# A transformer layer on one core: first gate weights in small tiles, stores ahead of loads at the hand-over, a quarter of x kept as fp32 in memory

## The chip, the cores and the metric

The kernel runs on one core of a Trainium2 chip. The metric is the device time of one execution in microseconds (us). The engines are TensorE (PE in the profile, its weight loads PEld), VectorE (DVE), ScalarE (ACT), GpSimd (POOL) and SyncE (SP), which only issues transfers. Each engine has its own instruction queue, worked off in the order of the program; the engines wait for one another by semaphores.

## The reference, cut to what matters

One encoder layer over 1024 tokens of width 1024, all in fp32:

```python
xn = rms_norm(x, norm_g)
qa, ka, va, za, qb, kb, vb, zb = split(xn @ w_in, 8 groups of 512 columns)
ya = subln(diff_attention(qknorm(qa), qknorm(ka), va)) * silu(za)     # 4 heads, dense, T5 bias
yb = neighbourhood_attention(qknorm(qb), qknorm(kb), vb) * silu(zb)   # 8 heads, 2-D window, learned bias
x  = x + concat(ya, yb) @ w_out
x  = x + sigmoid(x @ w_ple_gate) * (p @ w_ple_proj)
```

## The kernel before

**Precision.** Every large product is made of three TensorE passes in fp32r. A helper splits each operand into a high part (an ACT copy to fp32r) and a low part (a DVE subtraction of the high part from the operand) and multiplies high by high, high by low and low by high. So each tile that TensorE reads costs one ACT and one DVE instruction first.

**Stage 1, projections (0 to 307 us).** The six groups qa, ka, va, qb, kb, vb go as three pairs through a Strassen-like scheme: seven products of half-size blocks for each pair, on blocks and sums of x (A11, A12, A22, S1 to S4) and blocks and sums of w_in. `steps` lists 42 half-products, and the loop at the end of the function body makes one in each iteration `i` (`step_mm`, 24 matmuls, lines L232 to L234), evacuates the one before (`step_evac`), loads weight chunks eight ahead (`w_load`), splits two chunks (`w_split`: ACT L215, DVE L216; chunks `4+2i` and `5+2i`), and runs what `hooks[i]` holds. Hooks 0 to 10 are the work on x: norm, transposes on TensorE (`x_trans`, L368), the block sums and their splits (L357, L358, and on POOL L397), and the small product p @ w_ple_proj (`ple_mm`; its halves are evacuated with a factor 0.5, half 0 on ACT L314, half 1 on DVE L316). Block A21 of x isn't used by the scheme. It is only needed by the gate products later, so `x_trans` splits it for tokens 512 to 1023 (ACT L378, DVE L382; DVE writes a difference into the fp32 copy's own tile), stores both parts to memory, and `x_reload` brings them back, high part in iteration 37, low part in iteration 40.

**The order of transfers.** Nearly all transfers are issued by SP, in the order of the program; one that waits holds up all behind it. Stores are collected in `pst` and issued by `ple_st()`: before the hooks up to iteration 39, after them from iteration 40 on.

**The hand-over (iterations 37 to 43, around 270 to 335 us).** The hooks 35 to 41 load what the neighbourhood attention needs: K, the bias R, Q for the first unit (`load_q`, three transfers), V (`load_v`, three transfers a unit, of 48 or 64 KB each), and the weights of the gates. Gate columns come in eight groups of 128 (`zseq`): `z_load` loads a group's weights into `zraw`, `z_split` makes the high part on ACT (L542) and puts the low part (DVE L545) into the list `zl`, which `z_low()` works off; `z_mm` makes the products (L567 to L569) for tokens 0 to 511 and then 512 to 1023, the second half with A21. The first group's `zraw` lies in the pool of six 4 KB tiles (`TA`) that also holds the projections' results on their way to memory (`C`, `vah`, `sth`, `stl`); its low part is made in iteration 42, when `fill(24)` first calls `z_low()`.

**Stage 2 (307 to 500 us)** interleaves 32 units of neighbourhood attention (scores `na_s` L632, softmax `na_e`, transposes `na_t` L670, values `na_pv`) with the gate products, by the generator `z_stream` and `fill(n)`: 24 matmuls first, then the first unit's scores, six matmuls, the second unit's scores, six matmuls, then the first unit's transposes. Once 24 matmuls of a group are through, `z_stream` puts the next group's high split into ACT's queue. Gate results for the dense attention are stored to `uad`. **Stage 3** is the dense attention, **stage 4** the output projection and the last gate.

Of the kernel before, what the change touches and what calls it, by code (L numbers as in the profile page):

```python
# [7 lines left out]
F32 = mybir.dt.float32  # L8
F32R = mybir.dt.float32r
I32 = mybir.dt.int32  # L10
AF = mybir.ActivationFunctionType
OP = mybir.AluOpType
# [3 lines left out]
P = 128  # L16
# [8 lines left out]
COL = dict(qa=0, ka=512, va=1024, za=1536, qb=2048, kb=2560, vb=3072, zb=3584)  # L25
# [6 lines left out]
def ap_of(t, off, dims):  # L32
    return bass.AP(tensor=t.tensor, offset=t.offset + off, ap=[list(d) for d in dims])
# [7 lines left out]
def layer_kernel(ctx, tc, x, p, ngr, w_in, w_out, gains, lamv, t5p, rpbp, w_gate, w_ple,  # L41
# [9 lines left out]
    def nm(s):  # L51
        cnt[0] += 1
        return f"{s}_{cnt[0]}"

    def T8(shape, dt=F32, n="t8"):
        return sb.tile(shape, dt, name=nm(n), tag="b8", bufs=16)

    def T4(shape, dt=F32, n="t4"):
        return sb.tile(shape, dt, name=nm(n), tag="b4", bufs=8)

    def TA(shape, dt=F32, n="ta"):
        return sb.tile(shape, dt, name=nm(n), tag="a4", bufs=6)

    def T2(shape, dt=F32, n="t2"):
        return sb.tile(shape, dt, name=nm(n), tag="b2", bufs=NB2)
# [17 lines left out]
    def PS(shape, n="ps"):  # L83
        return psp.tile(shape, F32, name=nm(n), tag="ps", bufs=4)
# [4 lines left out]
    def DT(shape, dt=F32, n="d"):  # L89
        n = nm(n)  # L90
        return dr.tile(shape, dt, name=n, tag=n, bufs=1)

    def raw(a):
        return a.bitcast(F32) if a.dtype == F32R else a

    def ld(o, i):
        return nc.sync.dma_start(raw(o), raw(i))  # L97

    def st(o, i):
        return nc.sync.dma_start(raw(o), raw(i))  # L100
# [6 lines left out]
    act = nc.scalar.activation  # L107
    V = nc.vector
# [97 lines left out]
    def w_split(j):  # L206
        if j >= len(chunks):
            return
        pi, n, k = chunks[j]
        r = raws.pop(j)  # L210
        if n == "P1":
            tk["b11", k] = r
        w = T4([P, 2, 512], F32R, n="w")
        wts[chunks[j]] = w
        act(w[:, 0], r, AF.Copy)  # L215
        V.tensor_tensor(w[:, 1], r, w.bitcast(F32)[:, 0], op=OP.subtract)  # L216
# [73 lines left out]
    pst = []  # L290
# [11 lines left out]
    def ple_mm(t, c0=0, c1=2):  # L302
        h, l = phl[t]
        if c0 == 0:
            po[t] = TA([P, D], n="pp")
        o = po[t]
        for c in range(c0, c1):
            cs = slice(c * 512, c * 512 + 512)
            ps = PS([P, 512], "pps")
            for i, (a, w) in enumerate(((h, wph), (l, wph), (h, wpl))):  # L310
                for k in range(2):
                    mm(ps, a[:, k], w[:, k, cs], start=(i + k == 0), stop=(i + k == 3))
            if c == 0:
                act(o[:, cs], ps, AF.Copy, scale=0.5)  # L314
            else:
                V.tensor_scalar(o[:, cs], ps, 0.5, None, op0=OP.mult)  # L316
        if c1 == 2:
            pst.append(lambda: st(ppd[t], o))

    def ple_st():  # L320
        while pst:
            pst.pop(0)()


    XA = {}
    a21d = DT([P, 2, 4, 512], F32R, n="a21")

    def x_tiles(*names):
        for n in names:
# [25 lines left out]
    def split(n, ts, src, low):  # L355
        h, l = XA[n]
        act(h[:, :, ts], src, AF.Copy)  # L357
        low.tensor_tensor(l[:, :, ts], src, h.bitcast(F32)[:, :, ts], op=OP.subtract)  # L358

    def x_trans(t):  # L360
        hat = xhats.pop(t)
        u = t % 4
        ts = slice(u * P, u * P + P)
        pt = [PS([P, 4, P], "xtp") for _ in range(2)]
        for b in range(2):
            for k in range(4):
                kc = 4 * b + k
                nc.tensor.transpose(pt[b][:, k], hat[:, kc * P:(kc + 1) * P], idn)  # L368
        if t < 4:
            split("A11", ts, pt[0], V)  # L370
            split("A12", ts, pt[1], V)
            for b in range(2):
                act(xf[b][:, u], pt[b], AF.Copy)
            return
        s, a21 = xsum[0][:, u], xsum[1][:, u]
        act(a21, pt[0], AF.Copy)
        sp = TA([P, 2, 4, P], F32R, n="a21s")
        act(sp[:, 0], pt[0], AF.Copy)  # L378
        V.tensor_tensor(s, pt[1], a21, op=OP.add)
        split("A22", ts, pt[1], V)  # L380
        V.tensor_tensor(a21, xf[0][:, u], pt[0], op=OP.subtract)
        V.tensor_tensor(sp[:, 1], pt[0], sp.bitcast(F32)[:, 0], op=OP.subtract)  # L382
        split("S1", ts, s, V)
        V.tensor_tensor(s, s, xf[0][:, u], op=OP.subtract)
        pst.append(lambda: st(a21d[:, :, :, ts], sp))

    xsum = []
    xf = []
# [11 lines left out]
        ts, s = xv(t)  # L400
        split("S4", ts, s, V)

    XA["A21"] = []

    def x_reload(i):
        XA["A21"].append(T8([P, 4, 512], F32R, n="xr"))
        ld(XA["A21"][i], a21d[:, i])

    qkd = {n: (DT([4, P, S], F32R, n=n + "h"), DT([4, P, S], F32R, n=n + "l")) for n in ("qa", "ka", "qb", "kb")}
    vad = (DT([S, 512], F32R, n="vah"), DT([S, 512], F32R, n="val"))  # L410
# [118 lines left out]
    zraw = {}  # L529
    zw = {}  # L530

    def z_load(col, T=None):
        r = (T or T4)([P, 8, P], n="zraw")
        ld(r, w_in[:, col:col + P].rearrange("(k q) d -> q k d", q=P))
        zraw[col] = r

    def z_split(col, k0=0, k1=8):
        r = zraw[col]
        if k0 == 0:
            zw[col] = T8([P, 2, 8, P], F32R, n="zw")  # L540
        w = zw[col]
        act(w[:, 0, k0:k1], r[:, k0:k1], AF.Copy)  # L542

        def low():
            V.tensor_tensor(w[:, 1, k0:k1], r[:, k0:k1], w.bitcast(F32)[:, 0, k0:k1], op=OP.subtract)  # L545

        zl.append(low)

    zl = []
    zp = []  # L550

    def z_low():
        while zl:
            zl.pop(0)()
# [44 lines left out]
    def load_q(pr, R):  # L599
        q1 = T4([P, 2, 512], F32R, n="Q1")  # L600
        h, l = qkd["qb"]
        for (dst, s) in ((q1[0:64], h), (q1[64:128], h), (Q2[R][0:64], l)):
            ld(dst, s[pr, :, R * 512:(R + 1) * 512].rearrange("(h d) s -> d h s", h=2))
        qb[pr, R] = q1
# [104 lines left out]
    def na_consts_k():  # L709
        k = T8([P, 2, S], F32R, n="K2")  # L710
        for h in range(2):
            cast(k[64:128, h], pen)
        K2.append(k)
# [8 lines left out]
    def load_r0():  # L722
        t = T8([P, 2, 752], n="R0")
        Rt[0] = [t[:, h] for h in range(2)]
        for h in range(2):
            ld(t[:, h], ap_of(rpbp, h * 23 * 48 + 1, [[48, 8], [1, 16], [1, 752]]))
# [90 lines left out]
    def pre(i):  # L817
        if i >= len(units):
            return
        pr, R, j = units[i]  # L820
        if j == 0:
            if R == 0:
                load_q(pr, 1)
            elif pr + 1 < 4:
                load_q(pr + 1, 0)
        if (R, j) == (0, 2) and pr + 1 < 4:
            load_k(pr + 1)
        if (R, j) == (1, 2) and pr + 1 < 4:
            load_r(pr + 1)
        if i + 2 < len(units):  # L830
            load_v(*units[i + 2])
# [89 lines left out]
    def s7():  # L921
# [3 lines left out]
    NS = len(steps)  # L925
# [7 lines left out]
        30: lambda: u_load(30),  # L933
        31: lambda: u_load(31),
        NS - 7: lambda: (na_consts_k(), load_k(0)),
        NS - 5: lambda: (load_r0(), x_reload(0)),
        NS - 4: lambda: z_load(COL["zb"], TA),
        NS - 2: lambda: (na_consts_q(), load_q(0, 0), load_v(0, 0, 0), load_v(0, 0, 1), z_split(COL["zb"], 0, 4),
                         z_split(COL["zb"], 4, 8), x_reload(1)),
        NS - 1: lambda: (pre(0), z_load(COL["zb"] + P), na_consts_k()),  # L940
    }
    lam_in = []
    normed = []
    for i in range(len(steps) + 2):
        w_sum1(LA - 2 + 2 * i)
        w_sum1(LA - 1 + 2 * i)
        if i < len(steps):
            step_mm(i, 0, 2)
        ready, normed = normed, []
        got = step_evac(i - 1) if 0 < i <= len(steps) else None  # L950
        for n, t0, c, rs in ready:
            qk_norm2(c, rs)
        if got:
            n, t0, c = got
            if n[0] == "v":
                v_evac(n, t0, c)
            else:
                normed.append((n, t0, c, qk_norm1(c)[1]))
        w_sum2(LA - 2 + 2 * i)
        w_sum2(LA - 1 + 2 * i)  # L960
        w_load(LA + 2 * i)
        w_split(4 + 2 * i)
        w_load(LA + 1 + 2 * i)
        if i < NS - 2:
            ple_st()
        if i in hooks:
            hooks[i]()
        if i >= NS - 2:
            ple_st()
        if i < len(steps):  # L970
            step_mm(i, 2, 3)
        if i == len(steps):
            fill(24)
            na_s(*units[0])
            na_e(*units[0])
            na_n(*units[0])
        w_split(5 + 2 * i)
        if i < len(steps):
            step_mm(i, 3, 4)
        for n, t0, c, rs in ready:  # L980
            qk_trans(n, t0, c)
# [464 lines left out]
```

## Time and profile before

| what | value |
|---|---|
| median of 3 runs (lowest to highest) | 844.71 us (844.12 to 845.74) |
| the profiled execution's own time, and its span | 844.99 us, 843.2 us |
| PE busy | 785.1 us, 93% of the span |
| PEld, DVE, ACT, POOL busy | 649.3, 517.9, 435.4, 266.8 us |
| granted clock of TensorE, mean | 0.976 of full speed |
| chain that ended last | PE 65%, DMA 10%, DVE 9%, ACT 5%, issue 5%, POOL 4% |

TensorE is busy for most of the span; the span is its work, plus the times in which it waits, plus what it loses when its clock is at the lower level. Which wait is worth looking for is read from the views of its waits and of short stretches, further down.

### The profile page before, as it was taken

To read this page: it belongs to the slowest core of one execution; us is meant where nothing else is said; L and a number is where in the kernel's file an instruction comes from. 1 tells how busy PE (TensorE), PEld (TensorE's weight loads), DVE (VectorE), ACT (ScalarE), POOL (GpSimd) and SP (SyncE) were. 2 spreads that over 40 slices of the span, in tenths; PEclk is the share of its full clock that TensorE was granted. 3 is DMA by queue.
4 is the path that set the end of the run, shared out by engine and by line. 5 is a ranking of instruction groups with operands and counts; after the bars stand their busy time and mean duration, and the time that the engine had idled before them with its cause. 6 is when DMAs were issued, how large, how long until landed. Compare 5 with 4: busy or idle time off the path is not lost.

```text
span 843.2 us, 12192 instructions
## 1 busy us (share of the span) xinstructions
PE 785.1 (93%) x4242; PEld 649.3 (77%) x4242; DVE 517.9 (61%) x992; ACT 435.4 (52%) x812; POOL 266.8 (32%) x267
## 2 busy tenths in 40 slices
PE   7899799999989957998979998999999999999997
PEld 6677578888878845777758776888888878888886
DVE  4568895686997624554545568777777752732332
ACT  5755355255435422553544659898888961411220
POOL 1002453261555400010101014767767661200000
PEclk9999899999999987999998999999999999999999
DMA  8665551944688999666675748757685526323232
GB/s 327 271 205 174 184 185 62 316 130 130 178 279 239 220 266 272 151 162 190 173 186 163 213 163 239 211 157 212 188 233 139 176 92 245 138 75 100 76 99 88
DMA packets 120701, 154.03 MB, mean 183 GB/s; under 512 B 23832, under 2 KB 78776, under 8 KB 120384
## 3 DMA queue, kind: packets, MB, share of 16 engines
q1 hardware_dynamic: 118848, 147.49, 59.3%
q0 software_dynamic: 1792, 5.77, 2.2%
q8 instruction: 34, 0.56, 0.3%
q14 instruction: 27, 0.22, 0.1%
HBM read 106.01 MB, written 47.22 MB: 182 GB/s over the span
## 4 chain that ended last, share of the span: by engine, by line
PE 65%; DMA 10%; DVE 9%; ACT 5%; issue 5%; POOL 4%; SPq 3%; DVEq 0%; ACTq 0%; POOLq 0%
PE dsp L1053 6%; PE ips L232 5%; PE ips L234 5%; PE ips L233 5%; PE gps L1246 3%; PE gps L1248 3%; PE gps L1247 3%; DMA uad<-zth 3%; PE dtp L1095 3%; PE ntp L670 2%; PE zps L569 2%; PE zps L567 2%; PE zps L568 2%; SPq L97 2%; POOL qrs L425 2%
## 5 line engine op out<-in xcount | busy, mean ns | idle before, releaser
L233 PE MATMUL ips<-w,xh 128*128 128x512 f32 x336 | 131.8, 392 | 4.9 <-DVE w L216 4.9
L232 PE MATMUL ips<-w,xh 128*128 128x512 f32 x336 | 133.7, 398 | 1.9 <-ACT w L215 1.9
L234 PE MATMUL ips<-w,xl 128*128 128x512 f32 x336 | 131.6, 392 | 0.0
L1078 POOL TENSOR_TENSOR s<-s,s 128x1024 f32<-128x1024 f32 x32 | 77.1, 2408 | 57.3 <-ACT s L1077 55.5
L425 POOL TENSOR_TENSOR qrs<-qms,nhalf 128x16 f32<-128x16 f32 x16 | 51.7, 3233 | 93.0 <-DVE qms L423 93.0
L1063 DVE CUSTOM_DVE_ANT_0 s<-dsp,T 128x1024 f32<-128x1024 f32 x64 | 77.7, 1215 | 2.5 <-PE dsp L1053 2.5
L233 PEld LDWEIGHTS ips<-w,xh 128*128 128x128 f32 x336 | 63.6, 189 | 18.3 <-DVE w L216 5.9
L1065 ACT ACTIVATE s<-s,dm 128x1024 f32<-128x1024 f32 x64 | 73.3, 1146 | 4.6 <-DVE dm L1063 4.5
L232 PEld LDWEIGHTS ips<-w,xh 128*128 128x128 f32 x336 | 63.4, 189 | 15.4 <-ACT w L215 2.3
L1053 PE MATMUL dsp<-K,Q 128*128 128x512 f32 x256 | 69.6, 394 | 4.9 <-DVE dm L1063 4.3
L234 PEld LDWEIGHTS ips<-w,xl 128*128 128x128 f32 x336 | 63.5, 189 | 13.5
L1102 DVE TENSOR_TENSOR aTl<-dtp,aTh 128x512 fp32r<-128x512 f32 x64 | 44.2, 691 | 48.0 <-ACT aTh L1096 48.0
L701 POOL TENSOR_TENSOR yb<-nay,yb 128x128 fp32r<-128x128 f32 x32 | 15.8, 493 | 180.4 <-ACT yb L700 180.4
L216 DVE TENSOR_TENSOR w<-wraw,w 128x512 fp32r<-128x512 f32 x84 | 66.1, 815 | 4.8 <-ACT w L215 4.4
L1053 PEld LDWEIGHTS dsp<-K,Q 128*128 128x128 f32 x256 | 45.9, 189 | 14.7 <-issue 3.1
L672 ACT ACTIVATE PT<-ntp 96x768 f32<-96x768 f32 (+1 forms) x32 | 25.9, 810 | 60.5 <-PE ntp L670 60.5
L569 PE MATMUL zps<-xh,zw 128*128 128x512 f32 x96 | 39.9, 416 | 14.3 <-DVE zw L545 14.3
L215 ACT ACTIVATE w<-wraw 128x512 fp32r<-128x512 f32 x84 | 49.6, 624 | 4.7 <-DVE wraw L191 4.5
L1246 PE MATMUL gps<-wgh,x1h 128*128 128x512 f32 x128 | 50.5, 395 | 0.0
L1096 ACT ACTIVATE aTh<-dtp 128x512 fp32r<-128x512 f32 x64 | 38.0, 593 | 23.8 <-PE dtp L1095 23.7
L1248 PE MATMUL gps<-wgh,x1l 128*128 128x512 f32 x128 | 49.9, 390 | 0.0
L1247 PE MATMUL gps<-wgl,x1h 128*128 128x512 f32 x128 | 49.8, 389 | 0.0
(180 smaller groups left out, 1848.0 us busy)
## 6 DMA issues: line engine op xcount, KB each, us to landing
wraw<-in_w_in_dram SPq DMA_DIRECT2D x72, 256.0 KB
x<-in_x_dram SPq DMA_DIRECT2D x8, 512.0 KB
ppd<-pp SPq DMA_DIRECT2D x8, 512.0 KB
K<-kbh SPq DMA_DIRECT2D x8, 512.0 KB
zraw<-in_w_in_dram SPq DMA_DIRECT2D x8, 512.0 KB
Q<-qbh SPq DMA_DIRECT2D x16, 256.0 KB
Q<-qah SPq DMA_DIRECT2D x16, 256.0 KB
Q<-qal SPq DMA_DIRECT2D x16, 256.0 KB
```

What stands on the lines that cost most here:

```text
L216: V.tensor_tensor(w[:, 1], r, w.bitcast(F32)[:, 0], op=OP.subtract)
L232: mm(ps, lh[:, k, a:a + P], w[:, 0], start=(new and k == 0), stop=False, skip_group_check=cont)
L233: mm(ps, lh[:, k, a:a + P], w[:, 1], start=False, stop=False, skip_group_check=cont)
L234: mm(ps, ll[:, k, a:a + P], w[:, 0], start=False, stop=(k == 3), skip_group_check=cont)
L425: G.tensor_tensor(rs, ms, nhalf, op=OP.pow)
L1053: mm(ps[:, cs], q[g][:, m, u * P:(u + 1) * P], k[:, cs], start=(g == 0), stop=(g == 1))
L1063: V.tensor_tensor_reduce(out=s, in0=ps, in1=back(Td[h][:, :], 1919 - (896 - P * qt), [[-1, S]]), scale=-1.0, scalar=BIG, op0=OP.add, op1=O ...
L1065: act(s, s, AF.Exp, bias=mx, scale=-1.0, accum_out=z[:, m:m + 1])
L1078: G.tensor_tensor(s1, s1, s2, op=OP.add)
L1246: mm(ps, h[:, k], wh, start=(k == 0), stop=False)
L1247: mm(ps, h[:, k], wl, start=False, stop=False)
L1248: mm(ps, l[:, k], wh, start=False, stop=(k == 7))
```

## The change

- `x_trans` keeps A21 as one fp32 tile, stores that (half the bytes, queued before the sums are made) and doesn't split it. `x_reload` loads it once, in iteration 37. The new `x_resplit`, in iteration 41, makes the high part on ACT in two halves and puts the two low parts into `zl`.
- The first gate weights go into two 2 KB tiles of another pool (`T2`), by two transfers, and their low part is made in iteration 40.
- `ple_st()` stands before the hooks in every iteration.
- `w_split(5+2i)` stands before the hooks, no longer after the third quarter of the step's matmuls.
- For `t >= 4`, both halves of `ple_mm` are evacuated on ACT.
- The second `na_consts_k` moves from iteration 41 to 42.

```diff
-            if c == 0:
+            if c == 0 or t >= 4:
                 act(o[:, cs], ps, AF.Copy, scale=0.5)
...
-    a21d = DT([P, 2, 4, 512], F32R, n="a21")
+    a21d = DT([P, 4, 512], n="a21")
...
-        s, a21 = xsum[0][:, u], xsum[1][:, u]
+        s, d = xsum[0][:, u], xsum[1][:, u]
+        a21 = TA([P, 4, P], n="a21s")
         act(a21, pt[0], AF.Copy)
-        sp = TA([P, 2, 4, P], F32R, n="a21s")
-        act(sp[:, 0], pt[0], AF.Copy)
+        pst.append(lambda: st(a21d[:, :, ts], a21))
         V.tensor_tensor(s, pt[1], a21, op=OP.add)
         split("A22", ts, pt[1], V)
-        V.tensor_tensor(a21, xf[0][:, u], pt[0], op=OP.subtract)
-        V.tensor_tensor(sp[:, 1], pt[0], sp.bitcast(F32)[:, 0], op=OP.subtract)
+        V.tensor_tensor(d, xf[0][:, u], pt[0], op=OP.subtract)
         split("S1", ts, s, V)
         V.tensor_tensor(s, s, xf[0][:, u], op=OP.subtract)
-        pst.append(lambda: st(a21d[:, :, :, ts], sp))
...
-    def x_reload(i):
-        XA["A21"].append(T8([P, 4, 512], F32R, n="xr"))
-        ld(XA["A21"][i], a21d[:, i])
+    def x_reload():
+        r = T8([P, 4, 512], n="a21r")
+        ld(r, a21d)
+        XA["a21r"] = r
+
+    def x_resplit():
+        r = XA["a21r"]
+        XA["A21"] = (T8([P, 4, 512], F32R, n="xh"), T8([P, 4, 512], F32R, n="xl"))
+        h, l = XA["A21"]
+        for k in range(2):
+            ks = slice(2 * k, 2 * k + 2)
+            act(h[:, ks], r[:, ks], AF.Copy)
+            zl.append(lambda ks=ks: V.tensor_tensor(l[:, ks], r[:, ks], h.bitcast(F32)[:, ks], op=OP.subtract))
...
+        if small:
+            r = [T2([P, 4, P], n="zraw") for _ in range(2)]
+            for i in range(2):
+                ld(r[i], src[:, 4 * i:4 * i + 4])
+            zraw[col] = lambda a, b: r[a // 4][:, a % 4:(b - 1) % 4 + 1]
+            return
...
-        NS - 5: lambda: (load_r0(), x_reload(0)),
-        NS - 4: lambda: z_load(COL["zb"], TA),
+        NS - 5: lambda: (load_r0(), x_reload()),
+        NS - 4: lambda: z_load(COL["zb"], True),
         NS - 2: lambda: (na_consts_q(), load_q(0, 0), load_v(0, 0, 0), load_v(0, 0, 1), z_split(COL["zb"], 0, 4),
-                         z_split(COL["zb"], 4, 8), x_reload(1)),
-        NS - 1: lambda: (pre(0), z_load(COL["zb"] + P), na_consts_k()),
+                         z_split(COL["zb"], 4, 8), z_low()),
+        NS - 1: lambda: (pre(0), x_resplit(), z_load(COL["zb"] + P)),
+        NS: na_consts_k,
...
-        if i < NS - 2:
-            ple_st()
+        ple_st()
+        w_split(5 + 2 * i)
         if i in hooks:
             hooks[i]()
-        if i >= NS - 2:
-            ple_st()
...
-        w_split(5 + 2 * i)
         if i < len(steps):
             step_mm(i, 3, 4)
```

## Rows read from the trace of the kernel before

**Rows 1.** Waits of PE, whole span: who waited for whom, us in total, times, longest.

```profile
PE zps L569 <- DVE zw L545: 14.3, 1, 14.3
...
PE ips L233 <- DVE w L216: 4.9, 2, 3.5
```

**Rows 2.** Stretches A:B, length, busy us of PE, PEld, DVE, ACT, POOL, granted clock, DMA share, GB/s.

```profile
160.00:170.00 10.00, 10.00 (x45) 8.29 (x45) 6.04 (x6) 0.24 (x1) 2.56 (x2) 1.00 0.90 294
...
302.00:308.00 6.00, 5.37 (x24) 4.13 (x22) 1.42 (x2) 0.07 (x1) 0.00 (x0) 1.00 0.80 155
...
320.00:326.00 6.00, 4.32 (x10) 3.49 (x11) 2.22 (x3) 0.00 (x0) 0.00 (x0) 0.50 0.92 243
```

**Rows 3.** Timeline of the hand-over, all engines: start, length, instruction, count, idle time before it.

```profile
300.93 1.14 ACT L542 ACTIVATE zw<-zraw 128x512 fp32r<-128x512 f32 x2
301.06 1.23 DVE L482 TENSOR_TENSOR C<-C,vah 128x1024 f32<-128x1024 f32 x1 [2.15 <-ACT vah L481]
...
306.53 0.39 PE L234 MATMUL ips<-w,xl 128*128 128x512 f32 x1
...
315.18 1.06 ACT L481 ACTIVATE vah<-C 128x1024 fp32r<-128x1024 f32 x1 [13.11 <-DMA kah<-sth]
...
321.68 0.29 PEld L569 LDWEIGHTS zps<-xh,zw 128*128 128x128 f32 x1 [14.73 <-DVE zw L545]
```

**Rows 4.** Timeline of SP's transfers in the hand-over: start, length of the issue, count.

```profile
295.33 2.45 SPq L97 DMA_DIRECT2D Q<-qbh  x2
...
298.57 5.28 SPq L97 DMA_DIRECT2D Vw<-vb  x6
304.99 2.45 SPq L97 DMA_DIRECT2D xr<-a  x1
307.54 0.38 SPq L100 DMA_DIRECT2D kah<-sth  x1
...
313.77 4.04 SPq L97 DMA_DIRECT2D Vw<-vb  x3
318.31 1.19 SPq L97 DMA_DIRECT2D zraw<-in_w_in_dram  x1
```

**Rows 5.** Timeline where stage 2 begins, all engines.

```profile
330.22 0.62 ACT L542 ACTIVATE zw<-zraw 128x512 fp32r<-128x512 f32 x1
...
331.44 0.88 PE L632 MATMUL nsp<-K,Q 128*128 128x384 f32 x4
...
333.54 0.82 PE L670 MATMUL ntp<-idn,nas 128*96 128x128 f32 x6
```

**Rows 6.** Chain of waits, 230 to 400 us: start, us, what.

```profile
371.74 5.56 DMA Vw<-vb
```

**Rows 7.** Waits of SP's queue, 288 to 345 us.

```profile
SPq L97 <- DMA Q<-qbh: 1.1, 1, 1.1
```

**Rows 8.** Stretches of the work on x, columns as in rows 2.

```profile
83.00:93.00 10.00, 3.25 (x11) 1.82 (x10) 8.56 (x12) 5.66 (x10) 3.09 (x3) 0.78 0.76 243
93.00:108.00 15.00, 14.03 (x60) 10.99 (x59) 13.44 (x17) 5.14 (x10) 6.58 (x4) 0.92 0.37 117
```

**Rows 9.** Instructions of lines L382 and L316: count, ns least/median/most, first and last start.

```profile
L382 DVE TENSOR_TENSOR a21s<-xtp,a21s x4: 684/684/685, 56.0 to 87.4; 128x512 fp32r<-128x512 f32 x4
...
L316 DVE TENSOR_SCALAR pp<-pps x8: 683/692/692, 13.4 to 64.2; 128x512 f32<-128x512 f32 x8
```

**Rows 10.** Timeline of the work on x, all engines.

```profile
43.05 0.74 PE L312 MATMUL pps<-wph,ph 128*128 128x512 f32 x2 [0.53 <-ACT ph L298]
...
90.07 1.65 POOL L397 TENSOR_TENSOR xsum<-xf,xsum 128x512 f32<-128x512 f32 x1 [6.91 <-DVE xl L358]
90.51 1.75 DVE L216 TENSOR_TENSOR w<-wraw,w 128x512 fp32r<-128x512 f32 x1
```

**Rows 11.** Waits of DVE and a stretch of stage 2, 428 to 450 us.

```profile
DVE nay L695 <- DMA uad<-zth: 5.7, 1, 5.7
...
440.00:450.00 10.00, 7.97 (x41) 6.71 (x42) 4.76 (x17) 3.07 (x8) 0.91 (x2) 0.66 0.61 183
```

More of the change, by code (lines that the diff above doesn't have):

```diff
@@ L401, in x_split4 @@
         split("S4", ts, s, V)
-    XA["A21"] = []
-    def x_reload(i):
-        XA["A21"].append(T8([P, 4, 512], F32R, n="xr"))
-        ld(XA["A21"][i], a21d[:, i])
+    def x_reload():
[10 more added lines that the diff above has]
+            zl.append(lambda ks=ks: V.tensor_tensor(l[:, ks], r[:, ks], h.bitcast(F32)[:, ks], op=OP.subtract))
     qkd = {n: (DT([4, P, S], F32R, n=n + "h"), DT([4, P, S], F32R, n=n + "l")) for n in ("qa", "ka", "qb", "kb")}
@@ L530, in layer_kernel, with z_load @@
     zw = {}
[L532 to L535, printed above, removed]
+    def z_load(col, small=False):
+        src = w_in[:, col:col + P].rearrange("(k q) d -> q k d", q=P)
+        if small:
[4 more added lines that the diff above has]
+            return
+        r = T4([P, 8, P], n="zraw")
+        ld(r, src)
+        zraw[col] = lambda a, b: r[:, a:b]
     def z_split(col, k0=0, k1=8):
@@ L541, in z_split @@
         w = zw[col]
-        act(w[:, 0, k0:k1], r[:, k0:k1], AF.Copy)
+        act(w[:, 0, k0:k1], r(k0, k1), AF.Copy)
         def low():
-            V.tensor_tensor(w[:, 1, k0:k1], r[:, k0:k1], w.bitcast(F32)[:, 0, k0:k1], op=OP.subtract)
+            V.tensor_tensor(w[:, 1, k0:k1], r(k0, k1), w.bitcast(F32)[:, 0, k0:k1], op=OP.subtract)
         zl.append(low)
```

## The prediction

> **What bounds the kernel now.** The shares come first: TensorE is busy for 93% of the span, so a change pays where it takes away a wait of TensorE, or the lower clock that follows one. The waits of TensorE, sorted by length, name one place: 14.3 us for the low part of the first gate weights, once [rows 1]; the next is a third of it. [...] The timeline then tells why. The last projection matmul starts at 306.53. The high part of the gate weights has been ready since 302. The low part stands in DVE's queue behind the evacuation of the last projections, and that behind ACT's copy of `vah`, which waits 13.11 us for the store of `sth` to land, whose tile it gets [rows 3]. SP issued that store at 307.54, behind nine loads and the second load of A21 [rows 4], and ACT could go on at 315.18, 7.6 us later [rows 3]. So the hand-over is bound by the order of SP's queue and by a pool one tile too small, not by an engine.
>
> Stage 2 begins with a fixed order: 24 gate matmuls, first scores, six matmuls, second scores, six matmuls, first transposes. I take the start of these transposes, 333.54 [rows 5], as the mark at which before and after are compared.
>
> **The change part by part.**
>
> *First gate weights.* The low part moves to iteration 40, behind the copy's subtraction at 301.06 (1.23 us long) and the high part that ends at 302.07 [rows 3]: 1.23 + 2 x 0.69 (the shape of L382, [rows 9]) make it ready at about 303.7, 2.8 us before TensorE asks. If that cover is gone, each us past 306.5 costs one. The pool gets its sixth tile back, and the stores go first, so no projection copy waits for a landing of 307 or later. Then TensorE goes on without a break: 24 x 0.222 = 5.3, first scores 0.9, 12 x 0.222 = 2.7, second scores 0.9 (the second scores of before, [rows 5], for both), in all 9.8, and the transposes could start at 306.93 + 9.8 = 316.7. That is 16.8 us less than 333.54: the wait of 14.3 and what the matmuls after it lose at the lower clock.
>
> *What is late next.* When the first 24 matmuls are through, ACT's queue holds the second group's high split, and the exponentials of the first scores stand behind it. From that split to the transposes it was 333.54 - 330.22 = 3.3 us [rows 5]. The split needs the second group's weights, which SP loads behind everything else of iteration 41. SP's order after the change: four stores, the last of which has its data at 302.3 and is issued by 302.7; nine loads, 8.5 us in before (295.33 to 303.85); two stores, 0.8 (0.38 each); six loads, 7.3 (Q 295.33 to 298.57, V 4.04); then the weights [rows 4]. Part of these issues are waits for earlier transfers to land [rows 7]. At the price of a store's issue, 0.38 each, the 17 that lie ahead would take 6.5 us, and the weights would be issued at 309.2; with all waits as before, 302.7 + 8.5 + 0.8 + 7.3 = 319.3. I take 316.5, nearer the late end, because the loads are the same. A landing took 5.56 us for a V load of stage 2 [rows 6] and up to the 7.6 above; with the short one the weights are there at 322.1, the transposes start at 325.4. So TensorE waits again, some 8.7 us, but 8.1 us earlier than before. Bounds: no wait (316.7) and weights that land at 319.3 + 7.6 = 326.9 (transposes at 330.2).
>
> *The clock after this new wait.* After a wait of that kind the granted clock is at the lower level for a while: 0.92 over 15 us after the waits at 83 to 93 us, a loss of 1.2 us [rows 8]; 2.5 us after the long wait, which is what the 16.8 hold beyond the 14.3. The new wait lies between: 1.8. Without it, 0.
>
> *A21.* The load of 1 MB that SP issued at 304.99 goes; it held the stores for 2.45 us plus the 1.1 before it [rows 4, 7], which is in the sum above. Its split is added: two ACT copies of 1.06 and two DVE subtractions of 1.23 (the copy L481 and the subtraction L482 have this shape, [rows 3]). ACT has nothing to do there until the first 24 matmuls end at about 312.3; DVE comes to the subtractions behind the last projection's sum, ACT's copy and its subtraction, 306.93 + 1.23 + 1.06 + 1.23 = 310.5, and ends them at 312.9; the first product with A21 is due at 306.93 + 5.3 + 0.9 = 313.1. I take 0; without the cover, up to 1.2.
>
> *The work on x.* DVE is behind here: at 83 to 93 us it is busy for 8.56 of 10, at 93 to 108 for 13.44 of 15, while TensorE, waiting for weight splits [rows 1], has 3.25 of the first 10 [rows 8]. The change takes four L382 from DVE (0.68 each) and four L316 (0.69 each), together 5.5 us [rows 9]; the four L316 are over by 64.2, before that backlog; of the four L382, spread from 56.0 to 87.4, I count three, 2.0 us. The split that stands ahead now is the one that TensorE waits for at 85 to 92; but the next chunks are queued behind the evacuation of step 6 and its norm, so TensorE will wait there instead. Against it: at 43.05 TensorE waits for ACT's `ph` [rows 10], which now stands behind one more weight split (0.5 us), and DVE's `pl` likewise; about 1 us is lost there. Of 2.0 I take 1.5 as gain, as most of what is lost at 43 lies ahead of DVE's backlog; bounds -3.0 and +1.0.
>
> In the trace the weight split at 90.51 took 1.75 us, not the 0.68 of this shape, beside POOL's subtraction of 1.65 that began 0.44 earlier [rows 9, 10]. By that row, three such splits that no longer follow a POOL subtraction would make the gain up to 3.3 larger; hence the bound of -3.0, and I don't count on it, since another DVE instruction takes their place. [...]
>
> **Sum.** -16.8 (the wait and its clock) + 8.7 (the new wait) + 1.8 (its clock) - 1.5 (work on x) = -7.8. From the profiled execution's 844.99 that gives 837.2; it lies 0.28 above the median of the runs, so 837 for the median. Most of it is decided in one number, the landing of the second weights.
>
> **The rivals.**
>
> *No new wait.* The second weights land by 312: -16.8 - 1.5, 826.7. For it: 1 MB less to load, and stores that drain early; the bound of 309.2 comes near. Against it: the loads ahead are as many and as slow.
>
> *The second weights as late as ever.* Weights at 326.9, transposes at 330.2: -3.3 + 1.8 - 1.5 = -3.0, 842.0. The small V loads are the mechanism: at 302 to 308, when six of them (48 or 64 KB each) were what was left to move, the transfer engines were busy for 0.80 and moved 155 GB/s, and at 160 to 170 they moved 294 [rows 2]; the three of iteration 41 now stand directly ahead of the weights. [...]
>
> *The change doesn't do what it says.* The copy at iteration 40 still waits for a store that lands late, the first gate weights' low part comes after 306.5, and TensorE waits at the old place for as long as the old chain lasts: 845. Against it: the stores that this copy waits for were issued ahead of the load at 295.33 [rows 4], and the subtraction behind the copy starts at 301.06 [rows 3].
>
> *Slower.* In stage 2 a store of a gate result stands in SP's queue behind V loads, its tile isn't free, DVE's `nay` waits 5.7 us for it, and the clock falls (0.66 over 10 us, 3.4 us lost) [rows 11]: 9.1 us. It is one place now. If the earlier start lines up two more such stores with late loads, 18.2 us are added: 855. It decides from the second on; one more, 846, nearly cancels the gain. Against it: the loads ahead of those stores wait for tiles that the units free as they go, so they move with TensorE.
>
> **How the numbers follow.** Chances: forecast (834 to 839.5) 0.50; no new wait (826 to 832) 0.20; late as ever (839.5 to 843) 0.17; not what it says 0.05; slower 0.08. What a measurement of this kernel can tell from no change is about 0.2%, 1.7 us. Faster by more: 0.50 + 0.20 + 0.17 = 0.87; within: 0.05; slower: 0.08. Range 828 to 842.5: it cuts off half of the second case's lower part, and the last two, some 2 in 10.
>
> **What the profile after would show.** Right: the low part of the first gate weights by 305; no wait of TensorE at the first gate product, but one of 6 to 11 us at the first transposes, released through ACT's second gate split by a landing; transposes at 322 to 328; the A21 subtractions done before the product with A21; at 83 to 93 TensorE's waits for weight splits shorter, a new one a step or two later. Wrong: a wait at the first scores (Q late), at the product with A21, no wait at all, or longer waits at 390 or 435 than the one row shows.

## The result, and the profile after

The changed kernel takes 837.64 us (median of 7 runs, 834.66 to 840.36); the kernel before, beside it, 844.71 (843.89 to 848.11). The ratio is 0.9909, 95% interval [0.9886, 0.9932]. 837.0 had been predicted, with a range of 828 to 842.5. The profiled execution took 838.91 us, span 837.1 (before: 844.99 and 843.2). So the time came out as forecast. Whether it did so for the reasons given is another question, and the experiments answer it partly with no. Two executions of the experiments, of 1977.24 and 1100.61 us, fell in a slower state and are left out of the times below.

The waits of TensorE over the whole span, sorted by length, as in [rows 1]:

```profile
PE ntp L683 <- DVE nas L673: 20.4, 6, 11.5
PE dsp L1064 <- DVE dm L1074: 4.3, 4, 1.5
PE ips L232 <- DVE C L258: 4.1, 1, 4.1
```

The 14.3 us at the first gate product are gone; one of 11.5 at the first transposes has come. The timeline of the hand-over shows why (start, length, instruction, idle time before it), against [rows 3 to 5]:

```profile
298.60 1.23 DVE L488 TENSOR_TENSOR C<-C,vah 128x1024 f32<-128x1024 f32 x1 [1.19 <-ACT vah L487]
...
299.74 1.29 DVE L558 TENSOR_TENSOR zw<-zraw,zw 128x512 fp32r<-128x512 f32 x2
...
309.06 2.35 DVE L413 TENSOR_TENSOR xl<-a21r,xh 128x1024 fp32r<-128x1024 f32 x2
...
316.92 0.42 SPq L97 DMA_DIRECT2D zraw<-in_w_in_dram  x1
...
324.16 0.63 ACT L555 ACTIVATE zw<-zraw 128x512 fp32r<-128x512 f32 x1 [12.61 <-DMA zraw<-in_w_in_dram]
324.69 0.52 ACT L665 ACTIVATE nas<-nas,nam 128x288 f32<-128x288 f32 x1
...
326.48 1.51 PE L683 MATMUL ntp<-idn,nas 128*96 128x128 f32 x6 [11.55 <-DVE nas L673]
```

The first gate weights' low part (L558) is ready at 301.03, four us before TensorE asks. The second group's weights are issued at 316.92 and are there at 324.16; ACT's split of them stands ahead of the exponentials (L665), and TensorE waits for these. Two stretches, columns as in [rows 2]:

```profile
302.00:308.00 6.00, 6.00 (x28) 4.99 (x27) 2.70 (x4) 4.02 (x4) 0.00 (x0) 1.00 1.05 325
320.00:326.00 6.00, 0.00 (x0) 0.00 (x0) 0.14 (x1) 1.84 (x6) 0.00 (x0) 0.50 0.99 293
```

TensorE no longer stops at 302 to 308. At 320 to 326 it stands still, and the granted clock is 0.50.

### The profile page after: what moved, and what is told of

Read it like the earlier page. It is cut to its first block, busy times and chain, and to the rows that moved or that the text cites. A ratio compares the mean times of both kernels' runs of the same rounds, so it can differ in the third digit from the quotient of the medians.

```text
span 837.1 us, 12190 instructions
## 1 busy us (share of the span) xinstructions
PE 783.7 (94%) x4242; PEld 649.8 (78%) x4242; DVE 511.8 (61%) x986; ACT 437.6 (52%) x814; POOL 266.2 (32%) x267
## 4 chain that ended last, share of the span: by engine, by line
PE 71%; DVE 8%; DMA 7%; ACT 5%; issue 4%; SPq 2%; POOL 2%; ACTq 0%; DVEq 0%; POOLq 0%
PE ips L232 7%; PE ips L234 7%; PE ips L233 7%; PE dsp L1064 6%; PE gps L1259 3%; PE gps L1257 3%; PE gps L1258 3%; PE dtp L1106 3%; DMA uad<-zth 3%; PE ntp L683 3%; PE pps L312 2%; PE zps L580 2%; PE zps L582 2%; PE zps L581 2%; DMA Vw<-vb 2%
## 5 line engine op out<-in xcount | busy, mean ns | idle before, releaser
L1089 POOL TENSOR_TENSOR s<-s,s 128x1024 f32<-128x1024 f32 x32 | 77.0, 2408 | 56.9 <-ACT s L1088 52.3
L216 DVE TENSOR_TENSOR w<-wraw,w 128x512 fp32r<-128x512 f32 x84 | 62.2, 778 | 5.9 <-ACT w L215 5.4
L580 PE MATMUL zps<-xh,zw 128*128 128x512 f32 x128 | 54.3, 424 | 0.0
L582 PE MATMUL zps<-xh,zw 128*128 128x512 f32 x128 | 51.1, 399 | 0.0
L581 PE MATMUL zps<-xl,zw 128*128 128x512 f32 x128 | 51.0, 398 | 0.0
```

Of the source, the lines that this page charges most:

```text
L580: mm(ps, w[:, 0, kc], xh(kc, a, b), start=(kc == 0), stop=False)
L581: mm(ps, w[:, 0, kc], xl(kc, a, b), start=False, stop=False)
L582: mm(ps, w[:, 1, kc], xh(kc, a, b), start=False, stop=(kc == 7))
L1089: G.tensor_tensor(s1, s1, s2, op=OP.add)
```

## The experiments

Each is one edit of the changed kernel unless it says otherwise, and is compared with the kernel before on the same chip. The table gives the ratio of the times, and from the traces the start of the transposes of five units of stage 2. Executions whose code is the same up to iteration 39 start step 2 of the projections anywhere from 49.03 to 51.60 us and their last matmul anywhere from 302.72 to 305.75, so a difference of up to three us between two rows of the table says nothing; the pattern along a row does. "Stores as before" has its ratio from one set of executions and its units from a later one.

| kernel | ratio to before | unit 0 | unit 4 | unit 8 | unit 12 | unit 16 |
|---|---|---|---|---|---|---|
| before | 1 | 333.54 | 352.79 | 370.72 | 392.46 | 413.28 |
| changed | 0.9909 [0.9886, 0.9932] | 326.48 | 346.76 | 364.68 | 387.47 | 407.87 |
| weights first | 0.9938 [0.9914, 0.9961] | 321.88 | 342.73 | 360.65 | 388.36 | 408.65 |
| split late | 0.9921 [0.9901, 0.9940] | 315.18 | 342.17 | 360.78 | 387.56 | 408.38 |
| stores as before | 0.9888 [0.9871, 0.9906] | 324.44 | 344.52 | 362.45 | 386.28 | 407.86 |
| A21 as before | 0.9992 [0.9976, 1.0009] | 331.12 | 352.27 | 370.20 | 393.10 | 414.07 |
| stores on POOL | 0.9868 [0.9842, 0.9893] | 326.05 | 346.70 | 364.63 | 384.24 | 403.18 |
| stores on POOL, split late | 0.9859 [0.9828, 0.9890] | 312.40 | 339.60 | 357.93 | 377.56 | 403.51 |
| stores on POOL, weights at 40 | 0.9843 [0.9815, 0.9871] | 312.46 | 332.02 | 358.35 | 377.97 | 399.86 |
| the same, bias on POOL | 0.9867 [0.9849, 0.9886] | 314.28 | 333.26 | 360.58 | 380.21 | 401.12 |

### Is the landing of the second weights what decides?

Weights first:

```diff
-NS - 1: lambda: (pre(0), x_resplit(), z_load(COL["zb"] + P)),
+NS - 1: lambda: (z_load(COL["zb"] + P), pre(0), x_resplit()),
```

> The changed kernel, and in iteration 41 the load of the second group's gate weights is issued ahead of the loads of Q and V instead of behind them. Theory (SP's order sets the new wait): in the changed kernel these weights are issued at 316.92, behind loads that begin at 311.40, and land 7.2 us later; here they are issued near 311.4 and land near 318.6, TensorE's wait of 11.55 us at the first transposes shrinks to about 6, the end comes 5 to 6 us earlier: 832 for the median. Rival A (the landing is bound by the transfers in flight, not by the issue): issued earlier, landing at 322 to 324 all the same, 836 to 838. Rival B (Q or V, now behind the weights, take the wait's place): TensorE waits as long as before, at the second scores or at the first product with V, 837 to 839.

Split late:

```diff
-                if k in (8, 12) and i + 1 < len(zseq):
-                    z_split(..., k - 8, k - 4)
+                at = (8, 12) if i else (12, 15)
+                if k in at and i + 1 < len(zseq):
+                    b = 4 * at.index(k)
+                    z_split(..., b, b + 4)
```

> The changed kernel, and the two halves of the second group's high split stand after the 36th and 45th gate matmul of the first group instead of after the 24th and 36th, so that the exponentials of the first units don't stand behind it in ACT's queue; no load moves. Theory (the weights land at 324.1 and TensorE doesn't need them before the first group's 48 matmuls are through; only ACT's order makes it wait): the wait of 11.55 us at the first transposes goes, with the 1.4 that the lower clock costs after it, and a wait of up to 4 us comes back where the split now stands: 826 to 831. Rival (V, loaded by the same queue and issued from 303.89 to 310.08, lands as late as the weights): the wait moves to the first product with V and stays above 8 us, 834 to 838.

Measured: 841.23 and 838.74 us. The wait at the transposes shrank as the theory said, from 11.5 to 7.1 in the first; in the second it went, and 6.5 came back where the split now stands. Both are 4 us ahead of the changed kernel at units 4 and 8, and none of it is left at unit 12. The waits that end between 365 and 400 us, of the changed kernel and then of weights first (who waited for whom, us in total, times, longest):

```profile
ACT zth L586 <- DMA uad<-zth: 6.5, 1, 6.5
...
PE npv L698 <- ACT PT L685: 2.2, 1, 2.2
```

```profile
ACT zth L586 <- DMA uad<-zth: 11.4, 1, 11.4
...
PE npv L698 <- ACT PT L685: 7.1, 1, 7.1
```

ACT's tanh needs a tile whose store (uad) has not landed, and ACT's copy for the next product with V stands behind that tanh. What TensorE had gained at the hand-over it waits for here, to the us, and the granted clock is at 0.50 for 10.24 us instead of 3.41. The chain of waits has the store itself, in the changed kernel and in weights first (start, us, what):

```profile
372.39 11.63 DMA uad<-zth
```

```profile
374.98 9.93 DMA uad<-zth
```

It lands at 384.0 and 384.9, whether TensorE is early or late. SP's queue explains that. Here is when it issues the weights of the fifth group of gate columns, in the changed kernel, weights first, A21 as before (the next experiment), and the kernel before (start, length of the issue):

```profile
361.55 1.26 SPq L97 DMA_DIRECT2D zraw<-in_w_in_dram  x1
```

```profile
361.53 1.06 SPq L97 DMA_DIRECT2D zraw<-in_w_in_dram  x1
```

```profile
365.90 1.11 SPq L97 DMA_DIRECT2D zraw<-in_w_in_dram  x1
```

```profile
367.30 1.05 SPq L97 DMA_DIRECT2D zraw<-in_w_in_dram  x1
```

The first two agree, though their TensorE is 4 us apart. From the hand-over on SP's queue runs at a pace of its own: in the changed kernel 52 issues lie between the last projection matmul (305.09) and this one, and they hold the queue for 50.7 of the 56.5 us. Counted from that matmul, the load is issued after 56.2 to 56.9 us in the changed kernel, weights first, split late, and the two runs below that put the stores and the weight splits back, although the first transposes come anywhere from 9.7 to 21.4 us after it; with A21 as before it is 59.5, in the kernel before 60.8.

### What sets when that queue is through?

A21 kept in memory as its two parts, loaded in two pieces of 1 MB, as before the change; the rest of the change stays:

```diff
-a21d = DT([P, 4, 512], n="a21")
+a21d = DT([P, 2, 4, 512], F32R, n="a21")
...
+        V.tensor_tensor(sp[:, 1], pt[0], sp.bitcast(F32)[:, 0], op=OP.subtract)
...
-NS - 2: lambda: (..., z_low()),
-NS - 1: lambda: (pre(0), x_resplit(), z_load(COL["zb"] + P)),
+NS - 2: lambda: (..., z_low(), x_reload(1)),
+NS - 1: lambda: (pre(0), z_load(COL["zb"] + P)),
```

> The changed kernel with A21 kept in memory as its two parts again, as before the change: a copy and four subtractions more on ACT and DVE in the work on x, a load of 1 MB in the loads of iteration 40 behind V, and no split of A21 at the hand-over; the rest of the change stays. Theory (this edit carries two terms of the gain): the projections end about 1.4 us later, since DVE has its four subtractions back, and the load of 1 MB ahead of everything in iteration 41 keeps SP's queue back as it did before, so that the gate result's store that ends the stall near 384 lands about 3 us later: 840 to 843. Rival A (the edit is worth nothing at the hand-over): only the early part is lost, 838.5 to 839.5. Rival B (the load isn't there when the first product with A21 wants it): TensorE waits 3 us or more there, and the time may still be anything from 838 to 843, as the stall near 384 sets when it is given back.

Measured: 843.79 us. The whole gain is gone, and the intervals of 0.9992 and 0.9909 don't overlap. Its waits of TensorE at the hand-over, 300 to 335 us:

```profile
PE ntp L677 <- DVE nas L667: 7.2, 1, 7.2
PE zps L575 <- DMA xr<-a: 5.6, 1, 5.6
```

The first gate product doesn't wait here either. Early low part, small tiles and stores first are all in; the wait came back as 5.6 us for the 1 MB and 7.2 at the transposes. The projections end 1.32 us later than in the changed kernel. That alone would be within the spread, but from step 2 to their end they take 255.44 us, where all eight traces with the changed kernel's code up to iteration 39 take 253.66 to 254.28; DVE has its four subtractions back, and ACT a copy. SP's load of the fifth gate weights is issued 4.35 later (365.90 for 361.55): the same 1.3, and 3.0 for the 1 MB. The lower clock at the stall near 390 us lasts 6.83 us instead of 3.41.

The stores of iterations 40 and 41 behind the loads again:

```diff
-        ple_st()
+        if i < NS - 2:
+            ple_st()
         w_split(5 + 2 * i)
         if i in hooks:
             hooks[i]()
+        if i >= NS - 2:
+            ple_st()
```

> The changed kernel with the stores of iterations 40 and 41 behind the loads again, as before the change; all else as changed. Theory 1 (the stores' place is needed for the gain): a copy of the last projections waits again for a store behind nine loads to land, 5 us or more beyond 302.2, and as the split of A21 stands behind it on ACT and DVE, TensorE waits 3 to 8 us at the first product with A21: 839 to 845. Theory 2 (the sixth tile of the pool and the early low part are enough): no wait there, and the loads are issued some 2 us earlier, the second weights too: 835 to 838.

Measured: 836.02 us (835.71 to 837.35). A second execution of it, taken for its trace:

> The kernel with the stores of iterations 40 and 41 behind the loads, all else as changed, once more for its trace; its median was 836.3 against 837.6 for the changed kernel beside another set of runs. Theory 2 of that run (the sixth tile of the pool and the early low part are enough): no wait of TensorE at the first gate product or at the first product with A21, and the second weights issued 1 to 3 us before 316.92. Otherwise a wait of 3 us or more at the product with A21.

Its time was 837.95 us, and the waits of TensorE at 300 to 335 us were these:

```profile
PE zps L581 <- DVE xl L413: 3.7, 1, 3.7
PE ntp L683 <- DVE nas L673: 3.3, 1, 3.3
```

Theory 1 is right about the wait, 3.7 us at the product with A21, and wrong about the time. The second weights are issued at 315.08 instead of 316.92, so the other wait is shorter; unit 0 is 2 us earlier than in the changed kernel, and at unit 16 the two are level. The stores' place is worth nothing that these runs can tell.

The second weight split of each iteration back behind the work on x:

```diff
         ple_st()
-        w_split(5 + 2 * i)
         if i in hooks:
...
             na_n(*units[0])
+        w_split(5 + 2 * i)
```

> The changed kernel with the second weight split of each iteration back behind the work on x; all else as changed. The early part of the changed kernel is 1.44 us ahead of the kernel before when the projections end, though 1.63 behind at step 2. Theory 1 (the order is what gains there): the projections end 1 to 2 us later, 838.5 to 840. Theory 2 (the gain comes from the instructions taken from DVE, and the order only moves waits, with 1 us lost at 43 us): step 2 comes about 1.5 earlier and the projections end up to 1.5 us earlier, 836 to 838.

Measured: 837.81 us, ratio 0.9910 [0.9889, 0.9931]; the last projection matmul starts at 305.06, in the changed kernel at 305.09. Theory 2 by the time, though step 2 was only 0.86 earlier, which is within the spread. From step 2 to the end it takes 254.87 us, 0.6 to 1.2 more than the eight traces named above, so the new order gains something there, too little for the times to tell. Its DVE shows what the order does, first this kernel, then the changed one:

```profile
89.54 1.76 DVE L216 TENSOR_TENSOR w<-wraw,w 128x512 fp32r<-128x512 f32 x1
...
92.47 2.35 DVE L191 TENSOR_TENSOR wraw<-wraw,wraw 128x512 f32<-128x512 f32 x2 [1.17 <-POOL wraw L179]
```

```profile
93.08 2.35 DVE L191 TENSOR_TENSOR wraw<-wraw,wraw 128x512 f32<-128x512 f32 x2 [2.44 <-POOL wraw L179]
...
95.36 1.28 DVE L216 TENSOR_TENSOR w<-wraw,w 128x512 fp32r<-128x512 f32 x2
```

With the old order a split beside POOL's subtraction takes 1.76 us [rows 10]; with the new one both splits take 0.64, and DVE waits for POOL 1.27 us longer instead.

### Is it the stores' place, or the V loads?

The gate results' stores on POOL's queue:

```diff
-                    st(uad[(col - COL["za"]) // P][:, hf * 512:hf * 512 + 512], th)
+                    stp(uad[(col - COL["za"]) // P][:, hf * 512:hf * 512 + 512], th)
```

> The changed kernel, and the eight stores of gate results (uad) go through POOL's queue instead of SP's, so that they don't stand behind V loads; all else as changed. In the changed kernel the store issued at 372.39 lands 11.6 us later, ACT's tanh waits 6.5 us for its tile, TensorE waits and the clock falls at 387.99; where an experiment took 4.6 us out of the hand-over, this stall grew by as much (tanh waits 11.4, clock down for 10.24 us instead of 3.41). Theory (the stores' place among the V loads makes the stall): the time between the transposes of units 8 and 12, 22.8 us, falls to 18 to 19, the end comes 3 to 5 us earlier: 833 to 835. Rival (the transfer engines are what is late, whatever queue the store is in, or the next loads are late in its place): the stall stays within 1.5 us, 836 to 839.

Measured: 833.78 us, as the theory had it. Units 8 to 12 take 19.6 us instead of 22.8; no instruction waits for uad any more. The time to landing of these stores (us, least, median, most):

```profile
DMA to landing us min/median/max: 2.8/6.4/8.6
```

One load for a unit's V:

```diff
-        for m in range(3):
-            r0 = 4 * R + 4 * m
-            ld(v[0:4 * w, m], ap_of(vbd, ..., [[64 * 512, 4], [512, w], [1, P]]))
+        ld(v[0:4 * w], ap_of(vbw[R], ..., [[512, 4 * w], [4 * w * 512, 3], [1, P]]))
...
-                kv = k[:, h].rearrange("p (r c) -> p r c", c=64)[:, r0:r0 + 12, COL0[j]:COL0[j] + w]
+                kv = k[:, h].rearrange("p (r c) -> p c r", c=64)[:, COL0[j]:COL0[j] + w, r0:r0 + 12]
```

> The changed kernel with V kept in memory in two arrays in the order column, then row (12 rows each; the 8 shared rows are stored twice, 12 stores instead of 4), and the keys of a unit taken in that order, so that one load brings a unit's V (96 or 128 rows at a stride that one dimension tells) instead of three loads of 4 grid rows each; the scores read K at a stride of 64 elements and the bias at a stride. Theory (the three V loads per unit, slow to move and many to issue, set when everything behind them on SP's queue starts): the second weights are issued by 311 and land by 318, the wait of 11.55 us at the first transposes falls below 6, the stall between units 8 and 12 (22.8 us where 18 is undisturbed) goes: 826 to 832. Rival A (the bytes or the 512-byte pieces are the limit, which stay as they are): 835 to 839. Rival B (the strided reads cost TensorE or DVE more than the loads give back): the four score matmuls take longer than 0.88 us or the bias instruction longer than 0.55, slower than 839.

Measured: 849.01 us, ratio 1.0037 [1.0022, 1.0053]: rival B in the sum, and the theory in the stalls. At the hand-over the theory was missed by a little: the wait at the first transposes fell to 6.7 us, not below 6. SP's issues of V, in the changed kernel and in this one (count, ns least/median/most):

```profile
L97 SPq DMA_DIRECT2D Vw<-vb x96: 499/636/5388, 303.9 to 474.9; - x96
```

```profile
L97 SPq DMA_DIRECT2D Vw<-vbw x32: 323/471/1700, 307.5 to 465.0; - x32
```

Added up, V's issues hold SP's queue for 105 us of the changed kernel and 16 of this one. No wait of TensorE between 335 and 480 us is left over 0.4 us, and over 390 to 480 us its granted clock is 1.00, where the changed kernel's is 0.97. But the scores and the bias instruction, which now read at a stride, cost this, in the changed kernel and here (busy us, mean ns):

```profile
L660 DVE CUSTOM_DVE_ANT_1 nas<-nsp,R 128x384 f32<-128x384 f32 x32 | 16.4, 545 | 0.0
...
L645 PE MATMUL nsp<-K,Q 128*128 128x384 f32 x64 | 15.0, 360 | 0.0
```

```profile
L648 PE MATMUL nsp<-K,Q 128*128 128x384 f32 x64 | 28.4, 584 | 0.0
...
L663 DVE CUSTOM_DVE_ANT_1 nas<-nsp,R 128x384 f32<-128x384 f32 x32 | 24.5, 801 | 0.0
```

With the narrower shape, whose scores went from 11.2 to 22.3 us, TensorE has 24.5 us more to do; the end of the trace is 9.8 later, 3.35 of which are lost in the projections, between steps 18 and 24 (the twelve stores of V are new in that part; whether they are the cause wasn't tried). So the faster loads gave back some 24.5 - (9.8 - 3.35) = 18 us, an estimate that takes all of the 24.5 as added to the time.

Together with the late split:

> The V order and single load of the run before, together with the later place of the second group's high split. Theory (the loads were what gave back the 4.6 us that the later split had taken out of the hand-over): no wait over 2 us is left between 305 and 390, 824 to 829. Rival (what is left of the wait at the hand-over is short by then, the split's place doesn't matter): the same as the run before within 1 us.

Measured: 844.28 us, ratio 0.9980 [0.9958, 1.0002]. The level was missed, since the strided reads are in it; the difference to the run before is the answer: in the traces the transposes start 5.4 us earlier, and 4.9 of that are still there at the end. SP issues the fifth gate weights at 355.31 here and at 359.15 in the run before, so now that issue does move with TensorE. Where V doesn't hold the queue, a shorter hand-over is kept.

### How far it goes with the loads as they are

> The changed kernel with both the gate results' stores on POOL's queue and the later place of the second group's high split. Alone the first came to 833.8; the second alone took 4 to 10 us out of the hand-over up to unit 8 and gave all of it back in the stall near 384. Theory (that stall is what gave it back, and with the stores on POOL it is gone): 4 us and more are kept this time: 827 to 830.5. Rival (the V loads' pace gives it back at the next place): 833 to 835.

Measured: 833.07 us, no better than the stores on POOL alone, as the rival had it. The lead over those lasts to unit 12 and is gone at unit 16.

The second weights in iteration 40, behind Q:

```diff
-NS - 2: lambda: (na_consts_q(), load_q(0, 0), load_v(0, 0, 0), ...
-NS - 1: lambda: (pre(0), x_resplit(), z_load(COL["zb"] + P)),
+NS - 2: lambda: (na_consts_q(), load_q(0, 0), z_load(COL["zb"] + P), load_v(0, 0, 0), ...
+NS - 1: lambda: (pre(0), x_resplit()),
```

> The changed kernel with the gate results' stores on POOL's queue, and the load of the second group's weights in iteration 40, behind the three loads of Q and ahead of the six of V, instead of at the end of iteration 41. Theory (only the landing of these weights makes TensorE wait at the first transposes): issued near 304 they land by 312, the wait of 10 to 11.5 us goes with its lower clock, V for the first product comes half a us later than now; what is kept is at least what the later split keeps: 825 to 829. Rival (V, pushed back by 512 KB, is late at the first product with V, or the loads' pace gives the time back later): 830 to 834.

Measured: 831.13 us (830.40 to 831.84), the lowest median of all, in the rival's range. Its interval lies below that of the changed kernel, but overlaps those of the other kernels with the stores on POOL. No wait over 0.7 us is left at the hand-over. Unit 4 is 14.7 us ahead of the changed kernel (2.3 of it brought along from the projections), and unit 8 is 6.3 ahead, because DVE waits for the bias table R, which SP issues behind V loads (waits of DVE, 335 to 400 us):

```profile
DVE nas L660 <- DMA R<-in_rpb_dram: 10.9, 4, 5.4
```

With R on POOL's queue as well:

> The run before (the gate results' stores on POOL's queue, the second group's weights loaded in iteration 40) with the six loads of the bias table R of later heads on POOL's queue as well. In the run before TensorE was 14.7 us ahead of the changed kernel at unit 4 and 6.3 at unit 8: DVE waited 10.9 us for R, which SP issues at 345.84 behind V loads, and TensorE waited 12.3 us for DVE's scores. Theory (it is again the place in SP's queue): issued by POOL, R is there in time, the lead of 14.7 us falls to no less than 10 at unit 8, and 2 to 5 us more are kept at the end: 826 to 829. Rival (V loads themselves no longer keep up with TensorE, whatever stands among them): TensorE waits for V or Q instead, 830 to 832.

Measured: 833.55 us, no gain, and the wait that the rival named (waits of TensorE, 305 to 440 us):

```profile
PE npv L698 <- DMA Vw<-vb: 14.7, 7, 3.4
```

Nothing else stands in between now: TensorE waits for V itself.

## Why the prediction was right, and where it wasn't

*First gate weights: right.* Low part by 303.7 forecast, 301.03 measured; the third gate matmul starts 15.9 us earlier (305.77 for 321.68), without a wait. The sum's 0.222 us a matmul is 10 us over the 45 in the first line of [rows 2]; the first 24 gate matmuls took 5.44 us (305.31 to 310.75), 0.227 each, where the sum has 5.3.

*What is late next: right in place, cause and issue.* The weights' issue was taken at 316.5 and came at 316.92; the landing took 7.2 us instead of 5.56, the wait 11.55 instead of 8.7, the transposes start at 326.48 instead of 325.4.

*Its clock: right.* 1.8 forecast. The lower level lasts from 319.72 for 10.24 us, 3.5 of them with TensorE at work again, at a granted clock of 0.50: 1.7 lost, by estimate.

*The work on x: near in size by luck, half right in cause.* -1.5 forecast, and in the two profiled executions the last projection matmul starts 1.44 us earlier. But the eight traces with the changed kernel's code up to iteration 39 start it anywhere from 302.72 to 305.75 (before: 306.53, one trace). That spread lies ahead of step 2. In six of the eight, the changed kernel's own among them, the granted clock is at its lower level (0.50 in the changed kernel's own) for 3.41 us near 36 us, and step 2 starts at 50.32 to 51.60. In the other two, as in the kernel before, it isn't, and step 2 starts at 49.03 and 49.06 (before: 49.42), so the loss of 1 us forecast near 43 us isn't seen there. From step 2 to the end the eight take 253.66 to 254.28 us, the kernel before 257.11: about 3 us gained, twice the 1.5. By the two experiments 1.2 to 1.8 of that goes with A21 as one tile and 0.6 to 1.2 with the order of the splits; the rest wasn't tried. So the 1.44 is a larger gain less a later step 2, which goes with that lower clock and was in no term.

The waits for weight splits at 83 to 93 us went, and one of 4.1 for DVE's evacuation (C, L258) came behind them, as forecast. Of six splits of 1.75 to 1.78 us in the kernel before, the three at 78.98, 90.51 and 97.51 are short with the new order and three others stay long; DVE waits for POOL 1.27 us longer at two places instead. The forecast's reason not to count on the gain, that another DVE instruction takes the splits' place, isn't seen: between 60 and 140 us the longest of each DVE line takes at most 0.02 us more than before (C, L435: 2.32 for 2.30). The doubt itself was right for the most part: of up to 3.3 us, 0.6 to 1.2 is left.

*A21: right for the split, wrong for the edit.* The split cost nothing: the subtractions end at 311.41 and no product waits for them. But the load's absence was booked as part of what the stores' order brings at the hand-over. It is the edit without which nothing of the gain is left: with it undone and all else in, 0.9992. Whether it would bring the gain alone wasn't run.

*The step that failed* is "Most of it is decided in one number, the landing of the second weights", and with it the hand-over's -16.8 + 8.7 + 1.8 as the place of the gain. Runs that cut the new wait by 4.4 us, or moved it, ended no earlier. Up to unit 12 stage 2 goes as fast as SP's queue lets it. The load of the fifth gate weights is issued 5.75 us earlier than before (361.55 for 367.30): 1.44 by the end of the projections, and 4.3 that the queue needs less from there on, 3.0 of them for the missing 1 MB. Units 12 and 16 are 5.0 and 5.4 us ahead of before. That the sum came out near is luck as far as the runs show: at the first transposes it had -16.8 + 8.7 = -8.1 for the hand-over and 7.06 - 1.44 = 5.6 came, mostly because the new wait was 2.9 longer than forecast; what is kept further on is what the queue allows, and that happened to be as much.

*The rivals.* "No new wait" was built (weights at 40, with the stores on POOL): 831.1, not 826.7, and 2.7 less than with the stores on POOL alone, since V's pace gives most of it back. "As late as ever" named the right mechanism, V's loads, for the wrong place: their 96 issues, from 303.9 to 474.9 us, hold SP's queue for 105. With V in one load per unit the first two stores of gate results took 2.2 us (median) to land, the first of the changed kernel 11.63. But V's issues fell from 96 to 32 in the same edit, so it isn't shown whether the shape of the loads or their number makes the difference. "Slower" was no event of the changed kernel, and its mechanism is what ate the gain of weights first: the store of a gate result behind V loads. The argument against it, that the loads ahead of those stores move with TensorE, failed: TensorE came 4 us earlier, and the fifth gate weights were issued at 361.53 instead of 361.55.

*Open:* how much of V's 105 us on SP's queue is the number of issues and how much the slow landings behind which they wait. Not run: A21 as one tile alone on the kernel before, and the changed kernel without the first gate weights' small tiles and early low part, or with the four evacuations back on DVE. So it isn't shown what these parts are worth alone, or whether A21 needs them.

## What to carry to other kernels

Before you price a wait that is to go, look whether the queue that feeds the next stage is at its limit: if the same load is issued at the same us while the engine is 4 us earlier, the wait is only handed on, and what counts is what you take out of that queue. Test such a gain by undoing each part of the change alone: here the part whose own term was 0 turned out the one without which nothing was left. And follow a lead along the stage, unit by unit, in the trace; the place where it is lost names the next bound.

## What the runs showed of the hardware that was not expected

A matmul of 128x384 whose moving operand steps 64 elements instead of 1 took 584 ns on average instead of 360, and DVE's bias instruction of that width, reading at strides, 801 instead of 545. One store of 256 KB took 11.6 us to land behind V loads in SP's queue, 6.4 (median) on POOL's, and 2.2 (median of the first two) in SP's queue where V came in one load per unit.
